# One-hot matrices of the expert gates built row by row, and the late splits given to VectorE

## The chip, the cores and the metric

One core of one Trainium2 chip runs the whole program as one launch. The metric is the device time of a launch in microseconds (us). TensorE is called PE in the profile (its weight loads PEld), VectorE DVE, ScalarE ACT, GpSimd POOL, and the engine that issues most loads SP.

## The reference

A two-layer network over 256 tokens of 1024 features, followed by a second block. The part that matters here is the expert layer, which runs twice (layer 0 and layer 1). Every token has 8 heads with 16 chosen experts each, that is 128 entries of an expert index and a gate, out of 16384 = 128 x 128 experts:

```python
best, pos = lax.top_k(cand, K)
expert_idx = jnp.take_along_axis(cand_idx, pos, axis=-1)
gates = jax.nn.softmax(best, axis=-1)
u = expert_u[idx]
a = jax.nn.gelu(jnp.einsum('tkd,td->tk', u, xb)) * g
return jnp.einsum('tk,tkd->td', a, expert_v[idx])
```

## The kernel before

The kernel does not gather experts. It computes all 16384 activations for all tokens with dense products and multiplies them by a matrix of gates that is zero where an expert was not chosen. The weights of the first product (`pu`) come in 128 units per layer, each of 128 x 1024 float32; those of the second (`pv`) in 128 more.

Every unit takes the same path. SP loads it (`raw`), ACT copies it to the high part of `split` (L288), and DVE or POOL subtracts to get the low part (L290). Which of the two does so stands in a list that `plan` writes: the fourth field of a unit is true for POOL. `pump` issues these steps so that three split units are ahead of use. PE then runs 24 products of 128 x 256 per unit (L323 to L325: high by high, high by low, low by high). After a unit `tick` issues side work from the list `tasks`.

The `pu` units of a layer fall into two halves of 64, called the first and the second half below. In the second half the side work is `gating`, one step per unit (four units issue a second step in their middle). There are 64 blocks of 4 tokens, and step b does three things in this order:

- `scale(b-2)`: DVE multiplies 256 columns of the first half's activations `S` by the gates that PE made (L1164), ACT copies the rest to `stage` (L1168), and every fourth time POOL stores `stage` (L1170).
- `place(b-1)`: PE makes the gates of 4 tokens with 8 products of 128 x 128 in float16 (L1159), a burst of 8 between two units.
- `build(b)`: DVE makes the one-hot matrices of 4 tokens. `o1` has a one where the first index is (L1148), `og[:, 1]` where the second index is (L1149), and two multiplications by the high and the low part of the gate fill `og[:, 0]` and `og[:, 1]` (L1151).

The layout of these tiles is entry x 128 x 4 tokens, the tokens innermost, so PE reads the matrix of one token with a step of 4 elements (8 bytes). In the second half, `plan` gives every unit with i % 3 == 2 to POOL: 21 of 64 units per layer.

All engines take their instructions in the order of issue. On DVE that order in the second half is: the split of a unit if it is DVE's, then `scale`, then `build`.

Of the kernel before, what the change touches and what calls it, by code (L numbers as in the profile page):

```python
# [154 lines left out]
class Net:  # L155
# [14 lines left out]
    def shut(self, cm):  # L170
        cm.__exit__(None, None, None)

# [1 line left out]
    def tick(self, slots=1):  # L174
        for f in self.timed.pop(self.clock, ()):
            f()
# [16 lines left out]
        while self.tasks:  # L193
            self.tasks.popleft()()

# [1 line left out]
    def plan(self):  # L197
        a = self.a
        self.units = u = []

        def ws(src, tag, every=0):
            return [("w", src[i], tag, bool(every) and i % every == every - 1) for i in range(src.shape[0])]

        def on_pool(units, *which):
            return [(w[0], w[1], w[2], i in which) for i, w in enumerate(units)]

        def cols(l, lo, hi):
            return [("ada", (l, o)) for o in range(lo, hi)]

        def mix(units, jobs=(), per=1, skip=0):  # L210
            jobs = deque(jobs)
            for i, w in enumerate(units):
                u.append(w)
                for _ in range(per if i >= skip else 0):
                    if jobs:
                        u.append(jobs.popleft())
            u.extend(jobs)

        def spread(units, jobs, every, skip):
            jobs = deque(jobs)  # L220
            for i, w in enumerate(units):
                u.append(w)
                if i >= skip and i % every == 1 and jobs:
                    u.append(jobs.popleft())
            assert not jobs

        mk = ws(a["mem_k"], "mem_k")
        mix(on_pool(ws(a["mem_v"], "mem_v"), 2, 4, 6), cols(0, 0, 16), 2)
        mix(on_pool(ws(a["ret_qk"], "ret_qk"), 0, 1, 3))
        mix(ws(a["ret_g"], "ret_g") + ws(a["ret_v"], "ret_v"), cols(0, 16, 40))  # L230
        mix(ws(a["ret_o"], "ret_o"))
        mix(mk[:3])
        for l in range(2):
            pq = ws(a["pq"][16 * l:16 * l + 16], "pq")
            mix(on_pool(pq, 0, 1, 2, 4, 7, 10, 13))
            us = [("w", a["pu"][P * l + i], "pu", i % 4 == 3 if i < 64 else i % 3 == 2)
                  for i in range(P)]
            vs = [("w", a["pv"][P * l + i], "pv", False) for i in range(P)]
            mix(us)
            if l == 0:  # L240
                jobs = cols(0, 40, 48) + cols(1, 0, 37)
                spread(vs[:64], jobs[:17], 3, 13)
                spread(vs[64:], jobs[17:], 2, 9)
            else:
                mix(vs)
            if l == 0:
                mix(on_pool(mk[3:6], 2))
                mix(on_pool(ws(a["sgu_v"], "sgu_v"), 0, 1, 2) + on_pool(ws(a["sgu_u"], "sgu_u"), *range(0, 24, 4)), cols(1, 37, 48), 1, 6)
                mix(ws(a["sgu_o"], "sgu_o", 4))
                mix(mk[6:8])  # L250
        mix(ws(a["hy_v"], "hy_v") + ws(a["hy_qk"], "hy_qk", 2) + ws(a["hy_c"], "hy_c", 2))
        mix(ws(a["hy_oc"], "hy_oc", 2) + ws(a["hy_oa"], "hy_oa", 2))
        mix(ws(a["mem_q"], "mem_q", 2) + ws(a["mem_o"], "mem_o", 4))
        mix(ws(a["mlp_u"], "mlp_u") + ws(a["mlp_d"], "mlp_d"))
        self.n_load = self.n_split = self.w_done = self.w_split = 0
        self.raw = {}
        self.ring = deque()
        self.flying = [0, 0]
        self.split = deque()
# [53 lines left out]
            self.later.popleft()()  # L313

    def deepen(self):
        """More split units ahead of use, where there is room for them."""
        self.cm_deep, deep = self.pool("deep", bufs=DEEP_BUFS)
        self.ring = deque([deep] * DEEP_BUFS + [self.p_split] * SPLIT_BUFS)

# [1 line left out]
    def mm3(self, ps, w_hi, w_lo, x_hi, x_lo, start, stop, **kw):  # L321
        mm = self.nc.tensor.matmul
        mm(ps, w_hi, x_hi, start=start, stop=False, **kw)  # L323
# [11 lines left out]
            mid()  # L335

    def f1_pair(self, pss, tag, hs, shared=False, lag=0):
        """Two output chunks at a time, so that the first products keep pace with the features' arrival."""
        ws = [self.get(tag, k).rearrange("p s (c m) -> p s c m", m=P) for k in range(2)]
        for i in range(KC + lag):  # L340
            for j, c in ((0, i), (1, i - lag)):
                if 0 <= c < KC:
                    self.mm3(pss[j], ws[j][:, 0, c], ws[j][:, 1, c], hs[c][0], hs[c][1],
                             c == 0 and not (shared and j), c == KC - 1, skip_group_check=True)
# [45 lines left out]
            out += [(h[:, 0, j], h[:, 1, j]) for j in range(2)]  # L390
        return out

# [1 line left out]
    def ms_begin(self, total):  # L394
        self.ms_n, self.ms_total = 0, total
        self.ms_parts = []
# [15 lines left out]
            self.ms_parts.append(sq)  # L412

    def ms_part(self, pool, ns):
        """Squares of features that come in quick succession, summed on VectorE by the returned function."""
        sq = [pool.tile([P, T], F32, name=f"sqp{n}") for n in ns]
        for n, s in zip(ns, sq):
            self.nc.scalar.activation(s, self.x[:, n], AF.Square)
# [65 lines left out]
        v0, w = VEC[name]  # L484
        return self.vecs[:, v0 + i:v0 + (w if n is None else i + n)]

# [1 line left out]
    def out_proj(self, tag, hss, put, after):  # L488
        passes = len(hss)
        acc = self.accs("po")  # L490
# [26 lines left out]
            self.nc.vector.tensor_add(self.x[:, n], self.x[:, n], t)  # L517
        return put

# [1 line left out]
    def open_x(self):  # L521
        self.cm_x, self.p_n = self.pool("px")
        self.x = self.p_n.tile([P, KC, T], F32, tag="x", name="x")
# [6 lines left out]
    def run(self):  # L530
# [10 lines left out]
        self.vecs = c.tile([P, _off], F32, name="vecs")  # L541
        self.ones = c.tile([P, P], F32, name="ones")
        self.eps = c.tile([P, 1], F32, name="eps")
        self.iota_rep = c.tile([P, P, GT], F16, name="iota_rep")
        self.mod = [c.tile([P, 48], F32, name=f"mod{l}") for l in range(2)]
        self.d_c = self.p_d.tile([1, D], F32, name="d_c")
        self.d_mk = self.p_d.tile([P, KC, T], F32, name="d_mk")
# [31 lines left out]
        nc.gpsimd.dma_start(self.d_c, self.cact[0:1, :])  # L579
        self.ms_begin(KC)  # L580
        nc.vector.tensor_copy(self.iota, iota[:, :TOPK])
        nc.vector.tensor_copy(self.iota_rep, iota[:, :, None].to_broadcast([P, P, GT]))
        def squares(src, n):
            return lambda: [self.ms_add(src[:, n + k]) for k in range(4)]
        st = {}
# [20 lines left out]
        self.shut(self.cm_deep)  # L606
        self.shut(self.cm_x)

# [1 line left out]
    def mem_stats(self):  # L610
        r = self.rsqrt(self.ms_sum(), KC, "mrstd")
        self.nc.gpsimd.dma_start(self.d_mr, r)
# [32 lines left out]
            nc.gpsimd.dma_start(self.d_mk[:, n], o)  # L645

    def mem_reload(self, pool, queue):
        """The memory's split features once more."""
        nc = self.nc
        m = pool.tile([P, KC, T], F32, name="mem_again")  # L650
        for n in range(0, KC, 4):
# [7 lines left out]
        self.tasks.extend(one(n) for n in range(KC))  # L659
        return mh  # L660

# [1 line left out]
    def rope(self, pool, cs):  # L663
        nc = self.nc
        pi = pool.tile([P, T], I32, name="pi")
# [160 lines left out]
        self.shut(cm_a)  # L826
        self.load_keys(0)

# [1 line left out]
    def peer(self, l):  # L830
        nc, a = self.nc, self.a
        gain = self.mod_gain(l, "norm_ffn", 32)
# [11 lines left out]
        cm_s1, p1 = self.pool("s1")  # L844
        S1 = p1.tile([P, 64, T], F32, name="S1")
        cm_i, pi = self.pool("pi")
        i1 = pi.tile([P, T], F16, name="i1")
        i2 = pi.tile([P, T], F16, name="i2")
        g3 = pi.tile([P, 2, T], F16, name="g3")
        cm_r, pr = self.pool("rt", side="right")  # L850
        keys = self.keys
        self.routing_begin(pr, i1, i2, g3)
# [183 lines left out]
    def routing_rest(self, pr):  # L1036
# [5 lines left out]
        def block(tb):  # L1042
# [67 lines left out]
            def land():  # L1110
                pt, g3 = r["pt"], self.rt["g3"]
                nc.vector.tensor_copy(self.rt["i1"][:, tt], pt[:, 0:P])
                nc.vector.tensor_copy(self.rt["i2"][:, tt], pt[:, P:2 * P])
                gt = pt[:, 2 * P:3 * P]
                gr = pr.tile([P, P], F32, tag="gr", name="gr")
                nc.vector.tensor_copy(g3[:, 0, tt], gt)
                nc.vector.tensor_sub(gr, gt, g3[:, 0, tt])
                nc.vector.tensor_copy(g3[:, 1, tt], gr)

            for k in range(2):  # L1120
                add(lambda k=k: cand(k))
# [13 lines left out]
        for tb in range(2):  # L1135
            block(tb)

    # gates of one token as a 128 x 128 matrix: product of the one-hot rows of its 128 entries
    def gating(self, po, S, i1, i2, g3, d_g):
        nc = self.nc  # L1140
        made, mult, stage = {}, {}, {}

        def build(b):
            tt = slice(b * GT, b * GT + GT)
            sh = [P, P, GT]
            o1 = po.tile(sh, F16, tag="o1", name="o1")
            og = po.tile([P, 2, P, GT], F16, tag="og", name="og")
            nc.vector.tensor_tensor(o1, self.iota_rep, i1[:, None, tt].to_broadcast(sh), op=ALU.is_equal)  # L1148
            nc.vector.tensor_tensor(og[:, 1], self.iota_rep, i2[:, None, tt].to_broadcast(sh), op=ALU.is_equal)  # L1149
            for k in range(2):  # L1150
                nc.vector.tensor_tensor(og[:, k], og[:, 1], g3[:, k, None, tt].to_broadcast(sh), op=ALU.mult)  # L1151
            made[b] = (o1, og)

        def place(b):
            o1, og = made.pop(b)
            g = mult[b] = self.st_tile("g").rearrange("p (t c) -> p t c", t=GT)
            for t in range(GT):
                for k in range(2):
                    nc.tensor.matmul(g[:, t], o1[:, :, t], og[:, k, :, t], start=k == 0, stop=k == 1)  # L1159

        def scale(b):
            g = mult.pop(b).rearrange("p t c -> p c t")
# [38 lines left out]
            if q < 6:  # L1201
                self.tasks.append(lambda q=q: load(q + 2))

# [1 line left out]
    def sgu_load(self):  # L1205
        nc, a = self.nc, self.a
        self.cm_sw, p = self.pool("sgw")
# [144 lines left out]
        self.shut(cm_a)  # L1352
        self.shut(self.cm_sw)

# [1 line left out]
    def two_squares(self, pool, ns):  # L1356
        """Squares of the features before and after the gain of the norm that ends the first block."""
        nc = self.nc
        for n in ns:
            first = self.sq_acc is None  # L1360
# [443 lines left out]
```

## Time and profile before

| what | us |
|---|---|
| three runs | 2649.81, 2647.5, 2653.16; median 2649.81 |
| span of the profiled execution | 2652.8 |
| busy on PE, DVE, ACT, POOL in it | 2562.0, 1942.3, 1262.2, 474.9 |

The profile is of one execution; its span runs from the first to the last instruction, and its own time is given as this span alone. It is 3.0 us (0.11%) above the median of the runs. Busy time of an engine is time in which it had an instruction in work; "idle before, releaser" names what an engine was waiting for ahead of a group.

### The profile page before, as it was taken

The numbers are of one execution on the slowest core, as the hardware profiler recorded it, in microseconds if no ns is written. First come the engines' busy times: TensorE is split into PE (matmuls) and PEld (weight loads), VectorE is DVE, ScalarE is ACT, GpSimd is POOL, SyncE is SP. The second block draws the span as 40 slices with busy tenths as digits, with TensorE's granted clock in tenths as the row PEclk, the third lists the DMA queues.
The fourth block names the chain that finished last, engine by engine and source line by source line (L and its number), as shares of the span: only waits on it lengthen the run. The fifth ranks groups of instructions, "written<-read, shape, count | busy, mean of one in ns | idle before, by whom it ended". The sixth has DMA issues, their size and how long they took to land. (4 is left out here: it accounts for less than half of the span.)

```text
span 2652.8 us, 49924 instructions
## 1 busy us (share of the span) xinstructions
PE 2562.0 (97%) x20358; PEld 2495.4 (94%) x20358; DVE 1942.3 (73%) x3116; ACT 1262.2 (48%) x1774; POOL 474.9 (18%) x289
## 2 busy tenths in 40 slices
PE   5999999999999999999999999999999999889998
PEld 4989999999999999988999999999999999788998
DVE  8777688798868667775767887888675555785754
ACT  4445444444444445456545444444444445555643
POOL 5001312222211000020132122222100000552001
PEclk8999999999999999999999999999999999989999
DMA  7685556555569788867565665555675655434553
GB/s 283 227 299 165 189 175 188 179 171 169 170 199 318 253 300 272 274 228 233 167 207 164 183 183 178 169 171 174 241 249 183 217 184 175 143 118 153 175 186 117
DMA packets 146470, 532.54 MB, mean 201 GB/s; under 512 B 16096, under 2 KB 18272, under 8 KB 145344
## 3 DMA queue, kind: packets, MB, share of 16 engines
q1 hardware_dynamic: 133104, 481.36, 56.4%
q0 software_dynamic: 11648, 45.75, 4.7%
q8 instruction: 160, 2.62, 0.4%
q10 hardware_dynamic: 1488, 2.23, 0.2%
q14 instruction: 70, 0.57, 0.1%
HBM read 507.12 MB, written 22.16 MB: 200 GB/s over the span
## 5 line engine op out<-in xcount | busy, mean ns | idle before, releaser
L290 DVE TENSOR_TENSOR split<-raw,split 128x1024 fp32r<-128x1024 f32 x678 | 838.1, 1239 | 559.7 <-ACT split L288 558.0
L288 ACT ACTIVATE split<-raw 128x1024 fp32r<-128x1024 f32 x808 | 851.7, 1058 | 737.3 <-PE V L325 317.7
L323 PE MATMUL pu<-h,split 128*128 128x256 f32 x2496 | 719.6, 288 | 0.1
L324 PE MATMUL pu<-h,split 128*128 128x256 f32 x2496 | 707.7, 284 | 0.5 <-DVE h L383 0.5
L325 PE MATMUL pu<-h,split 128*128 128x256 f32 x2496 | 706.4, 283 | 1.1 <-POOL split L290 0.9
L325 PE MATMUL V<-a_sp,split 128*128 128x256 f32 x2048 | 580.8, 284 | 2.7 <-DVE split L290 2.7
L323 PE MATMUL V<-a_sp,split 128*128 128x256 f32 x2048 | 580.5, 283 | 1.1 <-ACT split L288 1.1
L324 PE MATMUL V<-a_sp,split 128*128 128x256 f32 x2048 | 580.8, 284 | 0.1
L290 POOL TENSOR_TENSOR split<-raw,split 128x1024 fp32r<-128x1024 f32 x130 | 329.7, 2537 | 850.2 <-ACT split L288 826.3
L323 PEld LDWEIGHTS pu<-h,split 128*128 128x128 f32 x2496 | 479.7, 192 | 0.9 <-ACT u L1325 0.3
L324 PEld LDWEIGHTS pu<-h,split 128*128 128x128 f32 x2496 | 478.2, 192 | 1.3 <-DVE h L383 0.7
L325 PEld LDWEIGHTS pu<-h,split 128*128 128x128 f32 x2496 | 477.4, 191 | 1.7 <-POOL split L290 1.3
L325 PEld LDWEIGHTS V<-a_sp,split 128*128 128x128 f32 x2048 | 393.5, 192 | 3.4 <-DVE split L290 3.3
L323 PEld LDWEIGHTS V<-a_sp,split 128*128 128x128 f32 x2048 | 393.5, 192 | 1.3 <-ACT split L288 1.3
L324 PEld LDWEIGHTS V<-a_sp,split 128*128 128x128 f32 x2048 | 393.4, 192 | 0.5 <-DVE a_sp L377 0.5
L881 ACT ACTIVATE S<-pu 128x512 f32<-128x512 f32 x128 | 76.6, 598 | 273.3 <-PE pu L325 273.3
L1151 DVE TENSOR_TENSOR og<-og,g 128x512 f16<-128x512 f16 x256 | 150.4, 588 | 8.8
L1159 PE MATMUL g<-og,o 128*128 128x128 f16 x1024 | 143.5, 296 | 1.4 <-DVE og L1151 1.4
L410 POOL TENSOR_TENSOR ms_acc<-ms_acc,sq 128x256 f32<-128x256 f32 x45 | 50.9, 1132 | 439.0 <-ACT sq L408 436.2
L295 DVE SCALAR_TENSOR_TENSOR raw<-raw,cact 128x1024 f32<-128x1024 f32 x96 | 126.9, 1328 | 2.0 <-ACT cact L578 0.7
L1159 PEld LDWEIGHTS <-o 128*128 128x128 f16 x1024 | 104.1, 118 | 9.9 <-issue 2.5
L323 PE MATMUL pq<-h,split 128*128 128x256 f32 x320 | 95.8, 299 | 3.3 <-ACT h L468 1.9
(377 smaller groups left out, 4097.8 us busy)
## 6 DMA issues: line engine op xcount, KB each, us to landing
raw<-in_pu SPq DMA_DIRECT2D x256, 512.0 KB, 3.6
raw<-in_pv SPq DMA_DIRECT2D x256, 512.0 KB, 4.2
raw<-in_ada SPq DMA_DIRECT2D x96, 512.0 KB, 4.6
raw<-in_pq SPq DMA_DIRECT2D x32, 512.0 KB, 3.9
d_g<-stage POOLq DMA_DIRECT2D x32, 512.0 KB, 3.9
g<-d_g POOLq DMA_DIRECT2D x16, 1024.0 KB, 9.0
raw<-in_mlp_u SPq DMA_DIRECT2D x32, 512.0 KB, 3.6
raw<-in_mlp_d SPq DMA_DIRECT2D x32, 512.0 KB, 4.2
```

Of the source, the lines that this page charges most:

```text
L288: nc.scalar.activation(s[:, 0], r, AF.Copy)
L290: eng.tensor_sub(s[:, 1], r, s[:, 0].bitcast(F32))
L295: nc.vector.scalar_tensor_tensor(r, r, 1.0, self.cact, op0=ALU.mult, op1=ALU.mult, accum_out=self.mod[l][:, o:o + 1])
L323: mm(ps, w_hi, x_hi, start=start, stop=False, **kw)
L324: mm(ps, w_hi, x_lo, start=False, stop=False, **kw)
L325: mm(ps, w_lo, x_hi, start=False, stop=stop, **kw)
L410: nc.gpsimd.tensor_add(self.ms_parts[0], self.ms_parts[0], sq)
L881: nc.scalar.activation(S[:, i - 1:i + 1], pt, AF.Gelu_apprx_tanh)
L1151: nc.vector.tensor_tensor(og[:, k], og[:, 1], g3[:, k, None, tt].to_broadcast(sh), op=ALU.mult)
L1159: nc.tensor.matmul(g[:, t], o1[:, :, t], og[:, k, :, t], start=k == 0, stop=k == 1)
```

## The change

- `build` makes the matrices token by token. Each token's `o1` is one comparison of a row of 128 numbers with a per-partition index; each of the two parts of `og` is one instruction that compares with the second index and multiplies by the gate. So 4 instructions of 512 elements become 12 of 128 elements, with one scalar per partition (`o1`) or two (`og`).
- The tiles hold each token's 128 columns next to each other, so PE reads them without a step.
- The indices and gate parts are float32 instead of float16 (they are scalars per partition now); the gate's parts still carry float16 values.
- `plan` gives no unit of the second half to POOL any more (the first half keeps i % 4 == 3).

```diff
-            us = [("w", a["pu"][P * l + i], "pu", i % 4 == 3 if i < 64 else i % 3 == 2)
-                  for i in range(P)]
+            us = [("w", a["pu"][P * l + i], "pu", i < 64 and i % 4 == 3) for i in range(P)]
...
-        self.iota_rep = c.tile([P, P, GT], F16, name="iota_rep")
+        self.iota_row = c.tile([P, P], F16, name="iota_row")
...
-        i1 = pi.tile([P, T], F16, name="i1")
-        i2 = pi.tile([P, T], F16, name="i2")
-        g3 = pi.tile([P, 2, T], F16, name="g3")
+        i1 = pi.tile([P, T], F32, name="i1")
+        i2 = pi.tile([P, T], F32, name="i2")
+        g3 = pi.tile([P, 2, T], F32, name="g3")
...
-            o1 = po.tile(sh, F16, tag="o1", name="o1")
-            og = po.tile([P, 2, P, GT], F16, tag="og", name="og")
-            nc.vector.tensor_tensor(o1, self.iota_rep, i1[:, None, tt].to_broadcast(sh), op=ALU.is_equal)
-            nc.vector.tensor_tensor(og[:, 1], self.iota_rep, i2[:, None, tt].to_broadcast(sh), op=ALU.is_equal)
-            for k in range(2):
-                nc.vector.tensor_tensor(og[:, k], og[:, 1], g3[:, k, None, tt].to_broadcast(sh), op=ALU.mult)
+            o1 = po.tile([P, GT, P], F16, tag="o1", name="o1")
+            og = po.tile([P, GT, 2, P], F16, tag="og", name="og")
+            for t in range(GT):
+                u = b * GT + t
+                nc.vector.tensor_scalar(o1[:, t], self.iota_row, i1[:, u:u + 1], None, op0=ALU.is_equal)
+                for k in range(2):
+                    nc.vector.tensor_scalar(og[:, t, k], self.iota_row, i2[:, u:u + 1], g3[:, k, u:u + 1],
+                                            op0=ALU.is_equal, op1=ALU.mult)
...
-                    nc.tensor.matmul(g[:, t], o1[:, :, t], og[:, k, :, t], start=k == 0, stop=k == 1)
+                    nc.tensor.matmul(g[:, t], o1[:, t], og[:, t, k], start=k == 0, stop=k == 1)
```

On DVE, in the second half of layer 0 before the change, two units follow each other, the first with its split on POOL (no L290 row), the second with its split on DVE:

```order
L1164 TENSOR_TENSOR S_2739<-S_2739,g 128x64x4
L1148 TENSOR_TENSOR o_6186<-iota_rep,i_2743 128x512
L1149 TENSOR_TENSOR og<-iota_rep,i_2744 128x512
L1151 TENSOR_TENSOR og<-og,g_2745 128x512 x2
L290 TENSOR_TENSOR split_6195<-raw_6050,split_6195 128x1024
L1164 TENSOR_TENSOR S_2739<-S_2739,g 128x64x4
L1148 TENSOR_TENSOR o_6234<-iota_rep,i_2743 128x512
```

On DVE in the changed kernel at the same place, one unit (L289 is the split, L1163 `scale`, L1147 and L1149 the build):

```order
L289 TENSOR_TENSOR split_6196<-raw_6026,split_6196 128x1024
L1163 TENSOR_TENSOR S_2739<-S_2739,g 128x64x4
L1147 TENSOR_SCALAR o_6234<-iota_row,i_2743 128x128
L1149 TENSOR_SCALAR og<-iota_row,i_2744,g_2745 128x128 x2
L1147 TENSOR_SCALAR o_6234<-iota_row,i_2743 128x128
L1149 TENSOR_SCALAR og<-iota_row,i_2744,g_2745 128x128 x2
L1147 TENSOR_SCALAR o_6234<-iota_row,i_2743 128x128
L1149 TENSOR_SCALAR og<-iota_row,i_2744,g_2745 128x128 x2
L1147 TENSOR_SCALAR o_6234<-iota_row,i_2743 128x128
L1149 TENSOR_SCALAR og<-iota_row,i_2744,g_2745 128x128 x2
L289 TENSOR_TENSOR split_6250<-raw_6083,split_6250 128x1024
```

Every unit's split now stands on DVE, ahead of `scale`, and 12 instructions stand where 4 stood. The order on PE does not move.

On POOL at this place before the change, splits and stores alternate; in the changed kernel only the stores are left:

```order
L290 TENSOR_TENSOR split_6146<-raw_6003,split_6146 128x1024
L1170 DMA d_g_86<-stage 128x1024
L290 TENSOR_TENSOR split_6290<-raw_6144,split_6290 128x1024
L1170 DMA d_g_86<-stage 128x1024
L290 TENSOR_TENSOR split_6449<-raw_6288,split_6449 128x1024
```

Over both layers 42 splits leave POOL for DVE.

## Rows read from the trace of the kernel before

**Rows 1.** The page, busy us of each engine (share of the span).

```profile
PE 2562.0 (97%) x20358; PEld 2495.4 (94%) x20358; DVE 1942.3 (73%) x3116; ACT 1262.2 (48%) x1774; POOL 474.9 (18%) x289
```

**Rows 2.** Stretches from the first to the last burst of gate products, layers 0 and 1.

```profile
core 0: us, PE busy (x) PEld busy (x) DVE busy (x) ACT busy (x) POOL busy (x), PEclk, DMA share, GB/s
531.10:762.10 231.00, 230.31 (x1922) 226.03 (x1920) 203.52 (x355) 95.74 (x150) 56.34 (x35) 1.00 0.53 171
1639.70:1871.00 231.30, 230.62 (x1922) 226.14 (x1920) 203.73 (x355) 95.74 (x150) 56.31 (x35) 1.00 0.53 171
```

**Rows 3.** Waits of PE: us in total, times, longest.

```profile
PE g L1159 <- DVE og L1151: 1.4, 8, 0.2
```

**Rows 4.** PE's timeline around two bursts: start, us, line, operands.

```profile
606.37 0.28 PE L325 MATMUL pu<-h,split 128*128 128x256 f32 x1
606.49 1.11 PE L1159 MATMUL g<-og,o 128*128 128x128 f16 x8
607.36 0.37 PE L323 MATMUL pu<-h,split 128*128 128x256 f32 x1
607.56 0.29 PE L324 MATMUL pu<-h,split 128*128 128x256 f32 x1
...
608.04 0.28 PE L325 MATMUL pu<-h,split 128*128 128x256 f32 x1
...
610.19 0.28 PE L325 MATMUL pu<-h,split 128*128 128x256 f32 x1
610.31 1.11 PE L1159 MATMUL g<-og,o 128*128 128x128 f16 x8
```

**Rows 5.** DVE's timeline in the same stretch.

```profile
604.00 1.23 DVE L290 TENSOR_TENSOR split<-raw,split 128x1024 fp32r<-128x1024 f32 x1
605.15 0.42 DVE L1164 TENSOR_TENSOR S<-S,g 128x256 f32<-128x256 f32 x1
605.48 0.42 DVE L1148 TENSOR_TENSOR o<-iota_rep,i 128x512 f16<-128x512 f16 x1
605.81 0.42 DVE L1149 TENSOR_TENSOR og<-iota_rep,i 128x512 f16<-128x512 f16 x1
606.27 0.89 DVE L1151 TENSOR_TENSOR og<-og,g 128x512 f16<-128x512 f16 x2
607.64 0.42 DVE L1164 TENSOR_TENSOR S<-S,g 128x256 f32<-128x256 f32 x1 [0.49 <-PE g L1159]
...
608.77 2.97 DVE L1151 TENSOR_TENSOR og<-og,g 128x512 f16<-128x512 f16 x2
```

**Rows 6.** Groups of DVE by form, window 531 to 766 us: count, busy us, mean ns.

```profile
L1151 DVE TENSOR_TENSOR og<-og,g 128x512 f16<-128x512 f16 x126 | 74.4, 590 | 4.3
L1148 DVE TENSOR_TENSOR o<-iota_rep,i 128x512 f16<-128x512 f16 x63 | 44.7, 710 | 0.0
L1149 DVE TENSOR_TENSOR og<-iota_rep,i 128x512 f16<-128x512 f16 x63 | 26.3, 418 | 0.0
```

**Rows 7.** DVE's timeline elsewhere: one-source instructions without, with one, with two scalars per partition.

```profile
489.02 0.22 DVE L1066 TENSOR_SCALAR ab<-pos 128x128 uint32<-128x128 uint32 x1
489.16 0.22 DVE L1067 TENSOR_SCALAR ab<-pos 128x128 uint32<-128x128 uint32 x1
...
31.61 0.29 DVE L691 TENSOR_SCALAR nturn<-nturn 128x256 f32<-128x256 f32 x1
31.82 1.22 DVE L295 SCALAR_TENSOR_TENSOR raw<-raw,cact 128x1024 f32<-128x1024 f32 x1
...
2430.11 0.62 DVE L1666 TENSOR_SCALAR p<-p,m 128x256 f32<-128x256 f32 x2
2430.64 1.22 DVE L290 TENSOR_TENSOR split<-raw,split 128x1024 fp32r<-128x1024 f32 x1
...
1262.96 1.52 DVE L1281 TENSOR_SCALAR v<-v,lnst 128x1024 f32<-128x1024 f32 x2
1264.41 1.21 DVE L290 TENSOR_TENSOR split<-raw,split 128x1024 fp32r<-128x1024 f32 x1
```

**Rows 8.** PE's timeline at products of 512 columns; six rows are left out.

```profile
1216.17 0.39 PE L356 MATMUL pv<-split,h 128*128 128x512 f32 x1
...
1217.79 0.39 PE L357 MATMUL pv<-split,h 128*128 128x512 f32 x1
```

More of the change, by code (lines that the diff above doesn't have):

```diff
@@ L581, in run @@
         nc.vector.tensor_copy(self.iota, iota[:, :TOPK])
-        nc.vector.tensor_copy(self.iota_rep, iota[:, :, None].to_broadcast([P, P, GT]))
+        nc.vector.tensor_copy(self.iota_row, iota)
         def squares(src, n):
@@ L1114, in land @@
                 gt = pt[:, 2 * P:3 * P]
[L1115 to L1118, printed above, removed]
+                gh = pr.tile([P, P], F16, tag="gh", name="gh")
+                nc.vector.tensor_copy(gh, gt)
+                nc.vector.tensor_copy(g3[:, 0, tt], gh)
+                nc.vector.tensor_sub(g3[:, 1, tt], gt, g3[:, 0, tt])
             for k in range(2):
@@ L1143, in build @@
         def build(b):
-            tt = slice(b * GT, b * GT + GT)
-            sh = [P, P, GT]
-            o1 = po.tile(sh, F16, tag="o1", name="o1")
-            og = po.tile([P, 2, P, GT], F16, tag="og", name="og")
-            nc.vector.tensor_tensor(o1, self.iota_rep, i1[:, None, tt].to_broadcast(sh), op=ALU.is_equal)
-            nc.vector.tensor_tensor(og[:, 1], self.iota_rep, i2[:, None, tt].to_broadcast(sh), op=ALU.is_equal)
-            for k in range(2):
-                nc.vector.tensor_tensor(og[:, k], og[:, 1], g3[:, k, None, tt].to_broadcast(sh), op=ALU.mult)
+            o1 = po.tile([P, GT, P], F16, tag="o1", name="o1")
[6 more added lines that the diff above has]
+                                            op0=ALU.is_equal, op1=ALU.mult)
             made[b] = (o1, og)
```

## The prediction

> **What bounds the kernel now.** The page first: PE is busy 97% of the span, DVE 73%, POOL 18% [rows 1]. So a change on DVE or POOL counts only where it makes PE wait, and a change on PE counts where nothing else takes over as the slowest. That is a question about the second half of the `pu` units, where the edited code runs. [...] PE is the bound here, but DVE stands close behind it, at 88% and not at the page's 73%.
>
> PE's timeline gives the price of a unit. Bursts start at 606.49 and 610.31, so a unit with its burst takes 3.82 us. From 608.04 to 610.19 there are 18 products in 2.15 us, 0.119 us each, so the 24 of a unit take 2.87 us and the burst of 8 takes the other 0.95 us, or 0.118 us a product, as much as a product of twice the columns [rows 4]. DVE's timeline gives the other side, from start to start since neighbours overlap: a split 1.15 us, `scale` 0.33 us, and the build from 605.48 to its end at 607.16, 1.68 us [rows 5]. With a split that is 3.16 us of 3.82 us. The 88% is higher than that because POOL's splits hold DVE up: the pair at L1151 took 2.97 us at 608.77 and 0.89 us at 606.27 [rows 5]; on average L1148 took 710 ns and L1151 590 ns, where L1149, the same size, took 418 ns [rows 6].
>
> **The change part by part.** *Splits.* 21 units per layer move from POOL to DVE, so all 60 units between the first and last burst cost DVE 1.15 us. In return POOL's holds go away; they are in DVE's busy time, not in its 3.16 us, so I simply rebuild DVE's work from undisturbed prices. The moved units are those of one list, and no DMA changes its place: SP loads in the same order, and POOL keeps its stores of `stage`, which get to their turn sooner. Behind a split on DVE wait `scale`, the build and so the next burst; that is the queue in which the cost below appears.
>
> *Build.* It becomes 4 instructions with one scalar per partition and 8 with two, of 128 float16 elements. The trace has no such instruction, so I put it together. Fixed part: one-source instructions with immediates start 0.14 us apart at 128 elements and 0.21 us at 256, so 0.07 us is fixed and 0.07 us is 128 elements of 4 bytes; a pair with one scalar per partition takes 0.53 us for 2 x 256 elements, so 0.265 - 0.137 = 0.13 us is fixed; a pair with two takes 1.45 us for 2 x 1024, so 0.725 - 0.547 = 0.18 us is fixed [rows 7]. Each scalar read costs 0.05 to 0.06 us. Stream: two-source float32 runs at (1.15 - 0.33) / 768 = 1.07 ns per element; two-source float16 takes the same 0.33 us for 512 elements as float32 for 256, half of that [rows 5]; one-source float32 is half of it too, 0.07 us per 128 elements [rows 7]. If both halvings hold together, 128 elements stream in 0.034 us. So 0.16 us and 0.215 us, and the build is 4 x 0.16 + 8 x 0.215 = 2.36 us. Bounds: 1.25 us if the scalars cost nothing (12 x 0.104), 2.8 us if only one halving holds, 3.6 us if none does. I take 2.36 us because the two scalar prices come from back-to-back instructions of the same kind, which is what the build is.
>
> [...]
>
> *DVE against PE.* From first to last burst DVE now has 63 scales and builds and 60 splits: 63 x (0.33 + 2.36) + 60 x 1.15 = 169.5 + 69.0 = 238.5 us. PE needs 231.0 us, or less if its burst gets cheaper. DVE is the longer of the two by 7.5 us. Part of it is absorbed once: today a build ends 3.1 us before its burst (607.16 against 610.31 [rows 4, 5]), and that lead is used up first. That leaves 4.5 us per layer, 9 us in all.
>
> *The reads without a step.* A product of 512 columns takes (1217.79 - 1216.17) / 7 = 0.231 us [rows 8], one of 256 columns 0.119 us, so a column costs 0.44 ns and one of 128 columns would take 0.064 us in place of 0.118 us. The burst would fall from 0.95 to 0.51 us, 28 us per layer. In the forecast this is worth nothing: PE waits for `og` instead, about 0.4 us at each burst. It pays only if DVE gets below PE. ACT is no third bound: 95.7 us busy of 231 us [rows 2].
>
> *The rest.* The smaller `iota_row`, the two tiles of indices and the five conversions at the end of routing lie under PE's work of the first half of the units; if that cover were gone they would cost below 1 us.
>
> The sum: 2652.8 us of span + 9 = 2661.8 us. The median of the runs shown lies 3.0 us below that span, so I forecast 2649.8 + 9 = 2659 us (+0.34%).
>
> **The rivals.** *Scalars are nearly free (faster).* If the scalars of the next instruction are fetched while the one before streams, the build is 1.25 us, DVE has 63 x 1.58 + 69.0 = 168.5 us, PE is the bound with a burst of 0.51 us, and the time falls by 2 x 28 = 56 us to 2594 us. For it: the short build has twelve equal instructions in a row. Against it: the pairs of rows 7 are such rows and pay in full [rows 7]. The point from which it decides: the build has to be below 2.29 us (0.19 us per instruction) to be no loss, and below 1.9 us to give PE all of its gain.
>
> *DVE is no bound and the step was no cost (no change).* If the build is below 2.29 us and a product of 128 columns still takes 0.118 us, the stretch is PE's 231 us as before: 2650 us. For it: a burst product could be held by its weight load, which is as wide as before. Against it: 0.118 us is just what 256 columns take [rows 4].
>
> [...]
>
> *The halvings do not combine (slower).* With 0.067 us of stream the build is 2.8 us: 63 x 3.13 + 69.0 - 231 - 3 = 32 us per layer, 2714 us. With 0.134 us it is 3.6 us and 2814 us. For it: no one-source float16 instruction stands in the trace. Against it: each halving does by itself [rows 5, 7].
>
> **How the numbers follow.** A measurement of this kernel tells about 0.2% (5 us) from no change. The forecast's mechanism, DVE at scalars' full price, gets 0.50; its own range is 2642 to 2676 us, since 0.01 us per instruction moves the build by 0.12 us and the time by 15 us. Of it 0.30 is slower by over 0.2%, 0.13 within 0.2%, 0.07 faster (a build a little cheaper than the sum, with some of PE's gain). Free scalars get 0.27, all faster; no bound and no gain 0.10, all within 0.2%; halvings that do not combine 0.13, slower. That makes faster 0.34, same 0.23, slower 0.43. The range takes in the free scalars and the forecast's own range and leaves out the last rival: 2590 to 2685 us.
>
> **What would show it.** In the profile after: the build's 512 instructions with one scalar (4 in each of 128 blocks) 0.16 us from start to start and its 1024 with two 0.215 us; DVE over 95% busy between first and last burst and that stretch some 235 us long; PE waiting for `og` at most bursts; burst products 0.064 us apart where PE does not wait. It is wrong if DVE shows idle time ahead of `scale` in most units (then the build was cheaper, and the stretch's length tells whether PE gained), or if a build instruction is above 0.25 us apart.

## The result and the profile after

The changed kernel takes 2667.24 us (median of 4 runs, 2665.01 to 2668.0) against 2649.77 us before: a ratio of 1.0060, 95% interval 1.0046 to 1.0074. It is slower by 17.5 us, on the side that was forecast and inside the range, but nearly twice the 9 us predicted. The profiled execution of the changed kernel stands for its runs (2665.5 us of span, 2667.3 us of time); the one of before, with 2652.8 us of span, was some 5 us above its median, if the same 1.8 us lie around it. So stretches are compared and not the two spans: they hardly vary (231.0 us in that execution, and 231.0 us again in an experiment below whose profiled run took 2646.6 us).

The page's first part, which answers to [rows 1]: busy us of each engine, its share of the span, instructions.

```profile
PE 2552.7 (96%) x20358; PEld 2458.2 (92%) x20358; DVE 2017.9 (76%) x4182; ACT 1266.0 (47%) x1774; POOL 373.3 (14%) x247
```

On this line little happened: PE 97% to 96%, DVE 73% to 76%. The windows from the first to the last burst of gate products, layers 0 and 1 (columns as in [rows 2]), show the whole of it:

```profile
core 0: us, PE busy (x) PEld busy (x) DVE busy (x) ACT busy (x) POOL busy (x), PEclk, DMA share, GB/s
529.90:769.30 239.40, 227.48 (x1923) 208.35 (x1922) 239.40 (x876) 97.20 (x150) 8.51 (x15) 0.99 0.50 162
1647.30:1886.80 239.50, 227.89 (x1922) 209.44 (x1920) 239.49 (x874) 97.04 (x150) 8.21 (x15) 0.98 0.50 162
```

DVE is busy in every microsecond of both (88% before, 203.52 of 231.00 us [rows 2]), PE no longer. PE's granted clock is 0.99 and 0.98 in place of 1.00: in layer 0 it is 0.96 from 560 to 600 us and from 680 to 720 us, and 1.00 outside these; as DVE leaves no gap, that is not what made the stretches longer. The stretches grew from 231.0 to 239.4 us and from 231.3 to 239.5 us: 8.4 + 8.2 = 16.6 us of the 17.5. The other 0.9 us is less than the runs of one kernel differ.

PE's waits for `og` over the whole program, which answer to [rows 3] (us in total, times, longest):

```profile
PE g L1158 <- DVE og L1149: 19.6, 116, 0.2
```

PE now waits 116 times, at 93 of the 128 bursts, where it waited 8 times. DVE's timeline over one unit answers to [rows 5] (L289 is the split, L1163 `scale`, L1147 and L1149 the build):

```profile
604.33 1.33 DVE L289 TENSOR_TENSOR split<-raw,split 128x1024 fp32r<-128x1024 f32 x1
605.47 0.53 DVE L1163 TENSOR_TENSOR S<-S,g 128x256 f32<-128x256 f32 x1
605.80 0.37 DVE L1147 TENSOR_SCALAR o<-iota_row,i 128x128 f16<-128x128 f16 x1
605.96 0.65 DVE L1149 TENSOR_SCALAR og<-iota_row,i,g 128x128 f16<-128x128 f16 x2
606.40 0.37 DVE L1147 TENSOR_SCALAR o<-iota_row,i 128x128 f16<-128x128 f16 x1
...
607.62 0.37 DVE L1147 TENSOR_SCALAR o<-iota_row,i 128x128 f16<-128x128 f16 x1
607.78 0.65 DVE L1149 TENSOR_SCALAR og<-iota_row,i,g 128x128 f16<-128x128 f16 x2
608.23 1.34 DVE L289 TENSOR_TENSOR split<-raw,split 128x1024 fp32r<-128x1024 f32 x1
```

Read it from start to start: the split 1.14 us, `scale` 0.33 us, one compare with one scalar 0.16 us, a pair with two scalars 0.44 us, the build 2.43 us (605.80 to 608.23), the unit 3.90 us. No row shows idle time ahead of it, and the next split starts where the build ends. The records are longer than the distances between their starts, so neighbours overlap; the durations of this execution can't be added up.

PE's timeline around the burst that this build feeds answers to [rows 4]:

```profile
607.56 0.53 PE L1158 MATMUL g<-og,o 128*128 128x128 f16 x6
608.27 0.44 PE L1158 MATMUL g<-og,o 128*128 128x128 f16 x2 [0.17 <-DVE og L1149]
608.51 0.36 PE L322 MATMUL pu<-h,split 128*128 128x256 f32 x1
608.72 0.28 PE L323 MATMUL pu<-h,split 128*128 128x256 f32 x1
```

Six products go at once, then PE waits for the last token's one-hots. From the first product of the burst to the second `pu` product behind it, 1.16 us pass; before it was 607.56 - 606.49 = 1.07 us [rows 4]. So PE's cheaper burst is used up in waiting, and a little more.

### The profile page after: what moved, and what is told of

Same layout as the page of the kernel before. It is cut to its first block, busy times and chain, and to the rows that moved or that the text cites. A ratio compares the mean times of both kernels' runs of the same rounds, so it can differ in the third digit from the quotient of the medians.

```text
span 2665.5 us, 50952 instructions
## 1 busy us (share of the span) xinstructions
PE 2552.7 (96%) x20358; PEld 2458.2 (92%) x20358; DVE 2017.9 (76%) x4182; ACT 1266.0 (47%) x1774; POOL 373.3 (14%) x247
## 4 chain that ended last, share of the span: by engine, by line
PE 65%; DVE 25%; DMA 4%; ACT 3%; issue 2%; POOL 1%; DVEq 0%; ACTq 0%; SPq 0%; POOLq 0%
PE V L323 8%; PE V L324 8%; PE V L322 8%; DVE og L1149 8%; DVE split L289 7%; PE pu L323 7%; PE pu L322 7%; PE pu L324 7%; DVE o L1147 3%; PE po L323 3%; PE po L324 3%; PE po L322 3%; ACT split L287 2%; DVE S L1163 1%; PE pq L323 1%
## 5 line engine op out<-in xcount | busy, mean ns | idle before, releaser
L289 DVE TENSOR_TENSOR split<-raw,split 128x1024 fp32r<-128x1024 f32 x720 | 902.8, 1257 | 519.5 <-ACT split L287 516.4
L289 POOL TENSOR_TENSOR split<-raw,split 128x1024 fp32r<-128x1024 f32 x88 | 228.6, 2598 | 621.3 <-ACT split L287 595.1
L1149 DVE TENSOR_SCALAR og<-iota_row,i,g 128x128 f16<-128x128 f16 x1024 | 310.3, 425 | 0.0
L1147 DVE TENSOR_SCALAR o<-iota_row,i 128x128 f16<-128x128 f16 x512 | 186.2, 364 | 0.0
L1167 ACT ACTIVATE stage<-g 128x256 f32<-128x256 f32 x128 | 49.3, 385 | 246.5 <-DVE S L1163 246.3
L1158 PE MATMUL g<-og,o 128*128 128x128 f16 x1024 | 125.1, 221 | 23.9 <-DVE og L1149 19.6
L1158 PEld LDWEIGHTS <-o 128*128 128x128 f16 x1024 | 68.5, 98 | 49.0 <-DVE o L1147 12.9
```

The source lines that it names most:

```text
L289: eng.tensor_sub(s[:, 1], r, s[:, 0].bitcast(F32))
L1147: nc.vector.tensor_scalar(o1[:, t], self.iota_row, i1[:, u:u + 1], None, op0=ALU.is_equal)
L1149: nc.vector.tensor_scalar(og[:, t, k], self.iota_row, i2[:, u:u + 1], g3[:, k, u:u + 1], op0=ALU.is_equal, op1=ALU.mult)
L1158: nc.tensor.matmul(g[:, t], o1[:, t], og[:, t, k], start=k == 0, stop=k == 1)
L1167: nc.scalar.activation(stage[0][:, :, k * GT:k * GT + GT], g[:, 64:], AF.Copy)
```

## The experiments

The theory: DVE is the bound between the bursts, and it is so because every scalar read from a partition costs it 0.05 to 0.06 us. The rivals: DVE became the bound for another reason (the moved splits, or the number of instructions and not their scalars), or PE's reads without a step gained nothing, so that nothing could have been won. Each kernel was timed beside the kernel before; of each, the stretch from the first to the last burst of layer 0 is given.

**The two parts apart.** The new build with the old plan of splits:

```diff
-            us = [("w", a["pu"][P * l + i], "pu", i < 64 and i % 4 == 3) for i in range(P)]
+            us = [("w", a["pu"][P * l + i], "pu", i % 4 == 3 if i < 64 else i % 3 == 2)
+                  for i in range(P)]
```

> The changed kernel, but every third late unit is split on POOL again. Theory (DVE is the bound, 3.90 us a unit): a POOL split takes 1.14 us off DVE in every third unit, but POOL's work holds one-source DVE instructions as it held the float16 ones (the 128x256 one at L1666 took 2.49 to 2.55 us beside POOL, 0.34 alone), about 2.1 us each time, so the stretch between first and last burst grows from 239 to about 260 us and the time from 2667 to about 2710 us. Rival (no hold on this kind of instruction): DVE has (2 x 3.90 + 2.76) / 3 = 3.52 us a unit, the stretch shrinks to about 217 us, the time to about 2623 us.

Measured: 2710.74 us, ratio 1.0227 (1.0208 to 1.0245), stretch 257.3 us. DVE's timeline in this kernel (L1148 and L1150 are its build):

```profile
604.35 0.53 DVE L1150 TENSOR_SCALAR og<-iota_row,i,g 128x128 f16<-128x128 f16 x2
...
605.41 0.25 DVE L1148 TENSOR_SCALAR o<-iota_row,i 128x128 f16<-128x128 f16 x1
605.57 2.61 DVE L1150 TENSOR_SCALAR og<-iota_row,i,g 128x128 f16<-128x128 f16 x2
608.10 0.24 DVE L1148 TENSOR_SCALAR o<-iota_row,i 128x128 f16<-128x128 f16 x1
```

And POOL's at the same time:

```profile
605.72 2.40 POOL L290 TENSOR_TENSOR split<-raw,split 128x1024 fp32r<-128x1024 f32 x1 [7.99 <-ACT split L288]
```

The pair at 604.35 takes 0.53 us. The one at 605.57 takes 2.61 us and ends about when POOL's split does (605.72 + 2.40 = 608.12): one-source instructions are held by POOL as the two-source ones were (before the change the pair at 608.77 took 2.97 us in place of 0.89 us [rows 5], while a split stood on POOL from 608.60 to 611.01 us). Such a hold costs DVE 2.08 us; a split of its own costs 1.14 us. So moving the splits was not what made the kernel slow; it saved 2710.74 - 2667.24 = 43.5 us of what the new build would have cost without it. The reverse, the old build with the new plan:

```diff
-            us = [("w", a["pu"][P * l + i], "pu", i % 4 == 3 if i < 64 else i % 3 == 2)
-                  for i in range(P)]
+            us = [("w", a["pu"][P * l + i], "pu", i < 64 and i % 4 == 3) for i in range(P)]
```

> The kernel before with the change of the plan alone: all late units are split on DVE, the build is the old one. Theory (the move costs nothing by itself): DVE has 1.14 + 0.33 + 1.68 = 3.15 us a unit, below PE's 3.82, the stretch stays 231 us, the time 2650 us within 0.2%. Rival (the 42 moved splits of 1.14 us are what made the change slower): some 8 us per layer more, 2665 us.

Measured: 2650.88 us, ratio 0.9998 (0.9988 to 1.0008), stretch 231.0 us. With the old build the 21 splits cost DVE less than it gets back from POOL's holds: DVE's busy time in the stretch falls from 203.5 us [rows 2] to 188.1 us. PE stays the bound, and the time doesn't move.

**The scalars.** The changed kernel with an immediate in place of the gate weight, for both parts (the gates are left out) and for the low part alone:

```diff
-                    nc.vector.tensor_scalar(og[:, t, k], self.iota_row, i2[:, u:u + 1], g3[:, k, u:u + 1],
+                    nc.vector.tensor_scalar(og[:, t, k], self.iota_row, i2[:, u:u + 1], 0.5,
```

> The changed kernel with the gate left out: the second scalar of the eight og instructions is the constant 0.5 in place of a value per partition. Theory (a scalar per partition costs 0.06 us and DVE is the bound): the eight fall from 0.223 to 0.163 us, the build from 2.43 to 1.96, the unit on DVE from 3.90 to 3.43 us, close to PE's 2.87 + 0.51; stretch about 211 us, time about 2610 us. Rival (the price lies in the number of instructions, not in the scalars): 0.223 us stays, 2667 us. Second rival (PE's burst is still 0.95 us where it does not wait): PE's 231 us bound it, 2650 us.

```diff
-                    nc.vector.tensor_scalar(og[:, t, k], self.iota_row, i2[:, u:u + 1], g3[:, k, u:u + 1],
-                                            op0=ALU.is_equal, op1=ALU.mult)
+                    nc.vector.tensor_scalar(og[:, t, k], self.iota_row, i2[:, u:u + 1],
+                                            0.5 if k else g3[:, k, u:u + 1], op0=ALU.is_equal, op1=ALU.mult)
```

> The changed kernel with one of the two gate parts left out: the low part's four instructions multiply by the constant 0.5. Theory (DVE is the bound and each scalar per partition costs 0.06 us): build 2.43 - 4 x 0.06 = 2.19 us, DVE 3.66 us a unit, stretch 63 x 2.52 + 60 x 1.135 - 2.6 = 224 us, time about 2667 - 2 x 15 = 2637 us, half way between the changed kernel and the run with both parts left out (2605 us). Rival (the gain comes at once when some point is passed): the time is at either end, 2667 or 2605 us.

Measured: 2604.88 us (0.9831, 0.9814 to 0.9849; stretch 209.5 us) with none, 2636.34 us (0.9947, 0.9929 to 0.9965; stretch 224.2 us) with half, 2667.24 us with all of the gate scalars. The number of instructions is the same in all three. DVE's timeline with half of them shows both prices side by side:

```profile
604.63 0.26 DVE L1147 TENSOR_SCALAR o<-iota_row,i 128x128 f16<-128x128 f16 x1
604.79 0.32 DVE L1149 TENSOR_SCALAR og<-iota_row,i,g 128x128 f16<-128x128 f16 x1
605.02 0.26 DVE L1149 TENSOR_SCALAR og<-iota_row,i 128x128 f16<-128x128 f16 x1
605.18 0.26 DVE L1147 TENSOR_SCALAR o<-iota_row,i 128x128 f16<-128x128 f16 x1
```

From start to start 0.16, 0.23 and 0.16 us: the same compare and multiply is 0.06 to 0.07 us cheaper when the gate is no scalar of the partition. That is 4 x 0.06 x 63 = 15 us per layer, and the stretch shrank by 239.4 - 224.2 = 15.2 us. The time follows the scalars one for one, as it does only while DVE is the bound. With none left, the stretch shrinks by another 14.7 us to 209.5 (the time by 31.5 us, after 30.9 us for the first half); DVE is still busy in all of it, and PE, with 207.16 of 209.70 us, is about level:

```profile
530.50:740.20 209.70, 207.16 (x1925) 200.80 (x1924) 209.70 (x878) 96.92 (x150) 8.27 (x15) 1.00 0.57 185
```

**PE's reads.** The kernel before, with its build, its plan and its number of products, but with products that read adjacent columns (which are other numbers than the gates need):

```diff
+            o1 = o1.rearrange("p c t -> p (c t)").rearrange("p (t c) -> p t c", t=GT)
+            og = og.rearrange("p k c t -> p (k c t)").rearrange("p (k t c) -> p k t c", k=2, t=GT)
...
-                    nc.tensor.matmul(g[:, t], o1[:, :, t], og[:, k, :, t], start=k == 0, stop=k == 1)
+                    nc.tensor.matmul(g[:, t], o1[:, t], og[:, k, t], start=k == 0, stop=k == 1)
```

> The kernel before, in which PE reads the same tiles without a step (the first 128 columns for the first token and so on, which are other numbers); DVE, POOL and ACT have the work of before. Theory (the step of 8 bytes doubled the product's time): the burst falls from 0.95 to about 0.5 us, the unit on PE to 3.38; DVE with POOL's holds needs about 3.4 us a unit and follows; stretch about 208 us, time about 2604 us. Rival (the step is free): 231 us and 2650 us.

Measured: 2605.76 us, ratio 0.9831 (0.9813 to 0.9849), stretch 208.3 us. PE's timeline at a burst:

```profile
605.50 0.62 PE L1161 MATMUL g<-og,o 128*128 128x128 f16 x8
605.93 0.36 PE L323 MATMUL pu<-h,split 128*128 128x256 f32 x1
606.13 0.28 PE L324 MATMUL pu<-h,split 128*128 128x256 f32 x1
```

From the burst's first product to the second `pu` product behind it: 0.63 us, where the stepped reads take 1.07 us [rows 4]. Less the 0.12 us of a `pu` product, the burst is 0.51 us. So the gain that the forecast counted as lost in waiting was there to be had: some 44 us with no other change. It is 231.0 - 208.3 = 22.7 us per layer, and not the 28 us that 0.44 us at 63 bursts come to. The list of waits for this stretch holds 5.5 us, where before the change it holds 0.7 us:

```profile
PE g L1161 <- DVE og L1151: 5.5, 8, 1.2
```

All of these waits stand at the bursts behind the four units that issue a second step in their middle. There two bursts start 1.94 us apart (535.58 and 533.64 the first time), DVE can't build that fast (`scale` and the build alone are 0.33 + 1.68 = 2.01 us [rows 5]), and PE waits at the next burst, though DVE has time to spare over the stretch as a whole (busy 200.70 of 208.40 us). Which of the two reads pays for its step was settled by giving the step to one operand at a time. First the weights alone (the changed kernel with the old build of `o1`; `iota_rep` is filled anew in each layer by one copy, here and in the next):

```diff
...
-            o1 = po.tile([P, GT, P], F16, tag="o1", name="o1")
+            tt = slice(b * GT, b * GT + GT)
+            sh = [P, P, GT]
+            o1 = po.tile(sh, F16, tag="o1", name="o1")
...
+            nc.vector.tensor_tensor(o1, self.iota_rep, i1[:, None, tt].to_broadcast(sh), op=ALU.is_equal)
...
-                nc.vector.tensor_scalar(o1[:, t], self.iota_row, i1[:, u:u + 1], None, op0=ALU.is_equal)
...
-                    nc.tensor.matmul(g[:, t], o1[:, t], og[:, t, k], start=k == 0, stop=k == 1)
+                    nc.tensor.matmul(g[:, t], o1[:, :, t], og[:, t, k], start=k == 0, stop=k == 1)
```

> The changed kernel with o1 alone built the old way, tokens innermost, so PE's weight loads read with a step of 8 bytes and its moving columns without. DVE: 0.335 + 8 x 0.223 = 2.12 us of build, 3.59 us a unit. If the weights' step is free, PE needs 3.38 us, DVE bounds, the stretch is 63 x 2.45 + 60 x 1.135 - 2.6 = 220 us and the time 2667 - 2 x 19.5 = 2628 us. If the weights' step is what doubled the products, PE has its 3.82 us, 231 us, 2650 us.

Then the moving columns alone (the kernel before with the new plan and the new build of `o1`):

```diff
...
-            o1 = po.tile(sh, F16, tag="o1", name="o1")
+            o1 = po.tile([P, GT, P], F16, tag="o1", name="o1")
...
-            nc.vector.tensor_tensor(o1, self.iota_rep, i1[:, None, tt].to_broadcast(sh), op=ALU.is_equal)
+            for t in range(GT):
+                u = b * GT + t
+                nc.vector.tensor_scalar(o1[:, t], self.iota_row, i1[:, u:u + 1], None, op0=ALU.is_equal)
...
-                    nc.tensor.matmul(g[:, t], o1[:, :, t], og[:, k, :, t], start=k == 0, stop=k == 1)
+                    nc.tensor.matmul(g[:, t], o1[:, t], og[:, k, :, t], start=k == 0, stop=k == 1)
```

> The reverse: o1 built row by row, og the old way, so only the moving columns are read with a step of 8 bytes. DVE: 0.65 + 1.25 = 1.90 us of build, 3.37 us a unit. If the moving step is free, PE needs 3.38 us, both are level, the stretch is about 210 us and the time about 2608 us. If the moving step is what doubled the products (the theory: the column is what PE streams), PE has 3.82 us, 231 us, 2650 us.

Measured: 2628.05 us (0.9911, 0.9895 to 0.9928; stretch 219.7 us) with stepped weights, 2650.34 us (0.9998, 0.9988 to 1.0008; stretch 230.8 us) with stepped columns. PE's timeline with stepped weights:

```profile
604.79 0.64 PE L1162 MATMUL g<-og,o 128*128 128x128 f16 x8
605.24 0.36 PE L322 MATMUL pu<-h,split 128*128 128x256 f32 x1
605.44 0.28 PE L323 MATMUL pu<-h,split 128*128 128x256 f32 x1
```

And with stepped moving columns:

```profile
604.96 1.08 PE L1162 MATMUL g<-og,o 128*128 128x128 f16 x8
605.80 0.37 PE L322 MATMUL pu<-h,split 128*128 128x256 f32 x1
606.00 0.28 PE L323 MATMUL pu<-h,split 128*128 128x256 f32 x1
```

From the burst's first product to the second `pu` product behind it, 0.65 us pass with stepped weights and 1.04 us with stepped columns, against 0.63 and 1.07 us with neither and both. The weights' step of 8 bytes costs 0.02 us a burst, and the doubling comes from the step of the moving columns.

**Two versions meant to beat both kernels.** The changed kernel in float32, with one weighted matrix and one product per token in place of a high and a low one:

```diff
...
-            o1 = po.tile([P, GT, P], F16, tag="o1", name="o1")
-            og = po.tile([P, GT, 2, P], F16, tag="og", name="og")
+            o1 = po.tile([P, GT, P], F32, tag="o1", name="o1")
+            og = po.tile([P, GT, P], F32, tag="og", name="og")
...
-                for k in range(2):
-                    nc.vector.tensor_scalar(og[:, t, k], self.iota_row, i2[:, u:u + 1], g3[:, k, u:u + 1],
-                                            op0=ALU.is_equal, op1=ALU.mult)
+                nc.vector.tensor_scalar(og[:, t], self.iota_row, i2[:, u:u + 1], g3[:, u:u + 1],
+                                        op0=ALU.is_equal, op1=ALU.mult)
...
-                for k in range(2):
-                    nc.tensor.matmul(g[:, t], o1[:, t], og[:, t, k], start=k == 0, stop=k == 1)
+                nc.tensor.matmul(g[:, t], o1[:, t], og[:, t], start=True, stop=True)
```

> The changed kernel with float32 one-hots: the gate stays one float32 value, so a token needs one weighted matrix and one product in place of two (no high and low part). DVE: four instructions with one scalar of 128 float32 (0.129 + 0.067 = 0.196 us) and four with two (0.190 + 0.067 = 0.257 us), a build of 1.81 us, 3.28 us a unit with split and scale. PE: four float32 products of 128 columns, which stand 0.110 us apart elsewhere in the trace (L1016), 0.44 us, so a unit of about 3.38 us. Theory (the changed kernel lost its gain on PE to the eight instructions with two scalars): PE is the bound again, the stretch is about 209 us, the time about 2606 us, faster than both kernels by 1.7% and more. Rival (float32 products with a new weight each are not as cheap between the other products, 0.2 us each): a unit as before, 3.8 us, 2650 us.

Measured: 2642.68 us, ratio 0.9973 (0.9958 to 0.9987), stretch 226.8 us: a miss, on PE's side. DVE's part came out as short as expected (L1144 and L1145 are its build):

```profile
604.32 0.34 DVE L1145 TENSOR_SCALAR og<-iota_row,i,g 128x128 f32<-128x128 f32 x1
604.57 0.28 DVE L1144 TENSOR_SCALAR o<-iota_row,i 128x128 f32<-128x128 f32 x1
604.77 0.34 DVE L1145 TENSOR_SCALAR og<-iota_row,i,g 128x128 f32<-128x128 f32 x1
606.00 1.23 DVE L289 TENSOR_TENSOR split<-raw,split 128x1024 fp32r<-128x1024 f32 x1 [0.89 <-ACT split L287]
```

The two kinds are 0.25 and 0.20 us apart, four of each per unit, and DVE waits 0.89 us behind them. PE's part did not. PE's timeline at a burst of 4 products:

```profile
603.95 1.06 PE L1153 MATMUL g<-og,o 128*128 128x128 f32 x8
604.76 0.36 PE L322 MATMUL pu<-h,split 128*128 128x256 f32 x1
604.96 0.28 PE L323 MATMUL pu<-h,split 128*128 128x256 f32 x1
```

Four products stand there as eight records, and the burst takes 1.01 - 0.12 = 0.89 us, 0.22 us for each float32 product. The 0.110 us of the expectation was one record: at L1016, too, a product is two of them (64 products in the program, 128 records in the trace). So the burst takes nearly the 0.95 us of the stepped float16 burst, PE is the bound again and little is gained.

The other version keeps the kernel before, moves the splits to DVE, and places the four tokens as two pairs, innermost, so that the columns of a token lie 4 bytes apart and not 8:

```diff
...
-            sh = [P, P, GT]
+            sh = [P, 2, P, 2]
+
+            def tok(x):
+                return x.rearrange("p (a t) -> p a t", t=2)[:, :, None, :].to_broadcast(sh)
...
-                nc.vector.tensor_tensor(og[:, k], og[:, 1], g3[:, k, None, tt].to_broadcast(sh), op=ALU.mult)
+                nc.vector.tensor_tensor(og[:, k], og[:, 1], tok(g3[:, k, tt]), op=ALU.mult)
...
-                    nc.tensor.matmul(g[:, t], o1[:, :, t], og[:, k, :, t], start=k == 0, stop=k == 1)
+                    nc.tensor.matmul(g[:, t], o1[:, t // 2, :, t % 2], og[:, k, t // 2, :, t % 2],
+                                     start=k == 0, stop=k == 1)
```

> The kernel before with all late units split on DVE and the tokens of a block innermost in pairs in place of fours, so PE's step is 4 bytes and DVE keeps four instructions of 512 elements whose innermost elements are neighbours. If DVE keeps its price, it has 3.07 to 3.15 us a unit. If a step of 4 bytes costs PE nothing, PE bounds at 3.38 us, the stretch is about 208 us and the time about 2604 us, faster than both kernels; if any step doubles the product, 231 us and 2650 us; if DVE's instructions lose their rate on rows of two, the build is about 2.6 us and the time about 2690 us.

Measured: 2603.44 us, ratio 0.9818 (0.9802 to 0.9834), stretch 207.7 us: faster than both kernels, by 48 us than the one before and by 64 us than the changed one. DVE's timeline over a unit (L289 the split, L1168 `scale`, L1151 to L1154 the build):

```profile
603.30 1.22 DVE L289 TENSOR_TENSOR split<-raw,split 128x1024 fp32r<-128x1024 f32 x1
604.43 0.41 DVE L1168 TENSOR_TENSOR S<-S,g 128x256 f32<-128x256 f32 x1
604.76 0.42 DVE L1151 TENSOR_TENSOR o<-iota_rep,i 128x512 f16<-128x512 f16 x1
605.10 0.42 DVE L1152 TENSOR_TENSOR og<-iota_rep,i 128x512 f16<-128x512 f16 x1
605.55 0.88 DVE L1154 TENSOR_TENSOR og<-og,g 128x512 f16<-128x512 f16 x2
607.04 1.23 DVE L289 TENSOR_TENSOR split<-raw,split 128x1024 fp32r<-128x1024 f32 x1 [0.60 <-ACT split L287]
```

And PE's at a burst:

```profile
604.99 0.63 PE L1162 MATMUL g<-og,o 128*128 128x128 f16 x8
605.43 0.36 PE L322 MATMUL pu<-h,split 128*128 128x256 f32 x1
605.63 0.28 PE L323 MATMUL pu<-h,split 128*128 128x256 f32 x1
```

The build is 605.55 + 0.88 - 604.76 = 1.67 us, as before the change, DVE has 0.60 us to spare in this unit, and PE passes from the burst's first product to the second `pu` product behind it in 0.64 us, as with adjacent columns (0.63 us).

## Why the prediction was right in kind and half in size

**What held.** DVE takes PE's place as the bound, at the full price of its scalars: shown by the stretch without idle time on DVE, and by the two kernels with fewer scalars, whose stretches shrink by just what DVE saves. The price of an instruction with one scalar was put at 0.16 us and is 0.16 us, so the two halvings of the stream do hold together for this kind, and that rival (2714 us) falls; the float32 version, with 0.20 us for the same instruction (0.13 us fixed and 0.067 us of stream in the prediction's terms), shows the second of them by itself. PE's burst without a step was put at 0.51 us, 0.064 us a product, and measures 0.51 us in the kernel that only changes PE's reads: 605.93 - 605.50 = 0.43 us for its eight products, about 0.055 us each, and 0.08 us by which the first `pu` product behind it is longer than 0.12 us. In the changed kernel it is hidden behind the waits, as forecast. ACT is no third bound (97 us busy of 239).

**The term that was mis-sized** is the build, and in it the instruction with two scalars. The prediction had 4 x 0.16 + 8 x 0.215 = 2.36 us; measured is 4 x 0.16 + 4 x 0.44 = 2.40 us from the rounded rows, and 2.43 us from the first start of the build to the next split. So these instructions are 0.22 us apart and a little more, and the fixed part put together from rows of 1024 float32 elements was 0.01 us too small. A part of that is rounding: with the split at 1.14 us, as measured, in place of 1.15 us, the 1.07 ns per element becomes 1.055 ns and the fixed part 0.185 us. By the prediction's own sum: 63 x (0.33 + 2.43) + 60 x 1.14 = 242.3 us of DVE, less 231 us and the 3 us of lead, is 8.3 us per layer; measured 8.4 and 8.2. With half of the scalars, too, it gives 63 x (0.33 + 4 x 0.16 + 4 x 0.39) + 60 x 1.14 - 3 = 225 us against 224.2. The error is 0.07 us per build, 63 builds and 2 layers, with no cover at all: when two near equal sums are subtracted (238.5 - 231), 1.6% of one of them is half of the difference. The prediction said that 0.01 us per instruction is worth 15 us; the 8 us missed are this sensitivity.

**Two errors that cancel, by luck.** Between the first and the last burst of a layer lie 59 units and not 60: of the 1922 records of PE in [rows 2], 63 x 8 are gate products, and the other 1418 are 59 x 24 and two at the window's edges. With 59 splits DVE's sum is 241.1 us, and it took 239.4 us, so the lead was worth 1.7 us and not 3. The prediction read it at one burst of the kernel before; in the changed kernel it was smaller from the first burst on:

```profile
528.98 1.22 DVE L289 TENSOR_TENSOR split<-raw,split 128x1024 fp32r<-128x1024 f32 x1
529.87 0.62 PE L1158 MATMUL g<-og,o 128*128 128x128 f16 x8
...
769.25 0.53 PE L1158 MATMUL g<-og,o 128*128 128x128 f16 x6
769.71 1.54 DVE L289 TENSOR_TENSOR split<-raw,split 128x1024 fp32r<-128x1024 f32 x1
```

These splits follow the builds of the first and of the last burst. DVE was done with the first 0.89 us ahead of its burst, and with the last 0.46 us after it had begun: together 1.35 us, most of the 1.7.

**Free scalars** (2594 us): refuted as a mechanism, since each scalar still costs 0.06 us in a row of twelve. The gain that it counted on is there, though it is 44 to 45 us and not 56: with the gate's scalars gone the time is 2604.88 us, with PE's reads alone changed 2605.76 us. (By the prediction's own sum PE's whole gain needs a build below 1.84 us, not 1.9 us.) Where operands are immediates, the prediction's estimate of the fixed part is 0.07 us [rows 7]; the run with half of the gate scalars shows 0.06 to 0.07 us more for each of them (0.23 us against 0.16 us from start to start).

**No bound, and the step was free** (2650 us): refuted on both counts, by the waits of the changed kernel (116, where there were 8) and by the burst up to the second `pu` product behind it, 1.07 us with the step and 0.63 us without. It was the step of the moving columns that cost time: the same passage took 1.04 us where they alone had the step of 8 bytes, and 0.64 us where both they and the weights had one of 4 bytes. For the weights the step of 8 bytes cost 0.02 us a burst.

**What the prediction left out** is that POOL also holds the new one-source instructions. It cost nothing, because the splits had left POOL, but it is why the new build can't go without that move: alone it gives 2710.74 us. Left out, too, is what two bursts in one unit cost PE, so its 28 us per layer for the reads were 5 us too many; in the forecast they counted for nothing.

**Left open:** why the last 0.9 us lies outside the two stretches, which these runs can't tell from nothing; and why the step of the columns costs PE time and that of the weights does not.

## What to carry to other kernels

When an edit takes work from the engine that is the bound and gives some to one that stands at 88%, sum up both engines over that stretch with prices from start to start, and test the sum against an error of 0.01 us per instruction: if that decides the sign, measure the instruction by itself first. Where work comes in clusters, as with two bursts in one unit, look at the waits there as well: a sum over the stretch does not show them. Look at the fixed part of an operation on few elements, and count the scalars read from a partition to it: here 0.13 of the 0.16 us of a compare with one scalar are fixed by the prediction's estimate, the gate as a second scalar cost 0.06 to 0.07 us, and twelve short instructions took 2.43 us for what four long ones do in 1.68 us. Ask also how much of a layout change is needed: here half the step (4 bytes in place of 8) gave PE the whole gain (0.64 us for the burst up to the second `pu` product, 0.63 us with adjacent columns) and left DVE's four instructions at their price (1.67 us, 1.68 us before).

## What was not expected of the hardware

- The step of the moving columns doubles a product of 128 float16 columns (burst 0.92 to 0.95 us at 8 bytes, 0.51 to 0.52 us at 4 or 2 bytes); the same step of the weights costs next to nothing (0.53 us).
- A float32 product of 128 columns is two records and 0.22 us, four float16 ones' time in the burst without a step.
- In the changed kernel's execution DVE's records grow along the stretch (the split from 1.22 us at the first burst over 1.33 us to 1.54 us at the last), while the distances of their starts stay the same (1.13 us from the first split's start to the next instruction's, 1.14 us at the other two). So this is no cost, and sums and means of busy time would have led astray. The kernel with stepped weights, with DVE as busy (219.80 of 219.80 us), shows a split of 1.21 us; the cause is open.
- The list of waits shows less than the waits cost: 19.6 us for both layers, where PE's unit grew from 24 x 0.119 + 0.51 = 3.37 us to 3.90 us, 0.53 us at each burst. A product's record lasts 0.22 us (median in the changed kernel), though in the kernel that only changes PE's reads the next one starts some 0.055 us after it, so a wait shows up by some 0.16 us too short, and a short one not at all.
